# A two-layer attention, RWKV and retention block: RWKV work moved up, its products kept adjacent, and the planner's durations replaced

## The chip, the cores and the metric

The kernel runs on one core of a Trainium2 chip. A core has five engines that run their own instruction streams: TensorE (PE, matmuls and transposes), VectorE (DVE), ScalarE (ACT), GpSimd (POOL) and SyncE (SP, which issues the transfers here). The metric is the device time of one execution in microseconds (us), as the median of several runs. One further execution was recorded by the hardware profiler; every duration and wait below comes from it.

## The reference

The input x has 256 tokens of 1024 numbers, in float32. Two layers run one after the other. Each layer is

```
h = rms(x) * norm1_g
aq, ak, av, rw, rq, rk, rv, rg, gates = split(h @ w_in)
o_a = sliding_window_attention(rms(aq)*g, rms(ak)*g, av, sinks) @ w_attn_o   # 8 heads, 2 kv heads, window 128
o_b = rwkv7_time_mix(rw, ...) @ w_rwkv_o                                     # 8 heads of 64
o_c = retention(rotary(rq), rotary(rk), rv, silu(rg)) @ w_ret_o              # 8 heads of 64
x = x + (sigmoid(gates) mixes o_a, o_b, o_c) @ w_out
x = x + (silu(h2 @ w_ffn_gate) * (h2 @ w_ffn_up)) @ w_ffn_down               # h2 = rms(x) * norm2_g
```

The RWKV branch keeps a 64x64 state S per head. With one step per token it computes S = S * w + (S a) b + v k and y = S r. The result is normalized per head, and then

```
y = y * lnx_g + lnx_b
y = (y + bonus) * g          # bonus = sum(r * k * r_k) * v,  g = sigmoid(gd) @ g2
```

## The kernel before

Tokens stand in two blocks of 128 (t = 0 and 1). Weights are streamed once, in 292 units of 512 KB (`wunit`). Each unit arrives by a transfer into `raw`; ScalarE rounds it into `wh`, VectorE forms the rest `wl = raw - wh`, and the big matmuls use both halves: three matmuls (`wh,hth`, `wl,hth`, `wh,htl`) for one product in higher precision. There are three buffers for each of raw, wh and wl. These big matmuls are called bulk. They are chained in program order: rq, rk and the other input projections first, then the gate projection gt, in between the output projections of attention (`po<-wh,oah` and its two companions), of retention (`po<-wh,och`) and of RWKV (`po<-wh,obh`), then w_out and the feed-forward part.

All else in a layer's first half, the mixer, is small work of three branches, each with a stream number: RWKV is stream 1, retention 2, attention 3, and gates with the mixing of the three outputs 4.

- Attention of a block: scores `pas`; VectorE adds the mask (`sc<-pas`), takes maxima (`amx`) and their negatives (`anm`); ScalarE forms exponentials; `adn` is their inverted sum; the normed scores are transposed (`ptp`) and multiplied by the values (`poa`), which gives `oah` and `oal` for the output projection.
- Retention of a block: `pst`, masked into `sT`, `po<-rv_sb,sT` and `po<-Rz,rqT`; then squares `rsq`, sums `rvr`, a power on GpSimd (`rrr`), two products into `o`, and transposes `ptc` that feed `och` and `ocl`.
- RWKV goes in chunks of 64 tokens. VectorE inverts 32x32 triangles in a loop of 31 steps, each a product `prod<-Y,Tt` and a sum `Tt<-Tt,prod`, and transposes the result into M and Tn; TensorE multiplies `pz<-Tn,GA` and `pm<-M,Zs`. Then four chunks follow one on the other: `pr` (state times inputs), `pu`, `pd` (the state's change), with copies and sums on ScalarE and VectorE in between (RS, SV, Sn), and `py`, whose sum is `ysb`. The end normalizes ysb, applies lnx, bonus and gate (`pgt`), and transposes (`pto`) into `obh` and `obl`.

The program does not issue instructions as it is written. It records every operation (`Program`), and a planner (`schedule`, `forward`) then lays them out by a list schedule: at each step it takes from the ready operations of the engine that is free first the one of highest priority. The priority is the longest path to the end (`bl`), from estimated durations (`cost`) and hand-over times (`LAT_*`), with classes above it for weight units that are due and for bulk. An operation whose tile finds no free buffer is parked. PSUM has four banks for bulk (`psg`) and four for small results (`pss`). `emit` (line 421, in the changed kernel 431) issues all instructions, so every row of the profile shows that line, and rows are told apart by their tiles. What the planner writes is one fixed order for each engine; on the chip each engine runs its own in that order and waits where an input isn't there.

Of the kernel before, what the change touches and what calls it, by code (L numbers as in the profile page):

```python
# [19 lines left out]
T = 256  # L20
# [87 lines left out]
class Program:  # L108
# [48 lines left out]
    def cost(self, eng, method, args, kw, out, ins):  # L157
        n = 1
        for _, c in list(out.ap)[1:]:
            n *= c  # L160
        if eng == "PE":
            if method == "transpose":
                return 109
            if kw["lhsT"].dtype == F32R:
                return 3 + n / 2.4
            c = max(4 + 4 * n / 2.4, 60)
            return c if out.ap[0][1] > 64 else (0.67 if out.ap[0][1] > 32 else 0.36) * c
        src = any(_psum(a) for a in ins)
        if eng == "DVE":
            if method == "reciprocal":  # L170
                return 69 + 6.3 * n
            if method == "tensor_reduce":
                n = 1
                for _, c in list(ins[0].ap)[1:]:
                    n *= c
            if method in ("tensor_copy", "tensor_scalar", "memset") and not src:
                return 69 + n / 1.92
            return 69 + n / 0.96
        if eng == "ACT":
            c = (51 if src else 94) + n / 1.2  # L180
            if _is_ap(kw.get("scale", 1.0)) or _is_ap(kw.get("bias", 0.0)):
                c += 25 if kw["func"] == AF.Copy and not src else 93
# [16 lines left out]
    def add(self, eng, method, fn, args, kw):  # L199
# [37 lines left out]
        if merged is not None:  # L237
            assert merged["eng"] == eng
            merged["calls"].append((fn, args, kw))
            merged["touch"].update(touched)  # L240
            merged["cost"] += cost
            return
        if self.bundle:
            self.bundle[0] = i
        self.ops.append(dict(eng=eng, calls=[(fn, args, kw)], preds=preds, touch=set(touched),
                             cost=cost, method=method, bulk=self.bulk and eng == "PE",
# [17 lines left out]
    def schedule(self):  # L264
# [15 lines left out]
        for i in range(n - 1, -1, -1):  # L280
            bl[i] = ops[i]["cost"] + max((bl[j] + l for j, l in succ[i]), default=0.0)
        return self.forward(succ, need, bl)

    def forward(self, succ, need, bl):
# [12 lines left out]
        ready = {e: [] for e in wait}  # L297
        parked = {}
        tfree = {e: 0.0 for e in wait}
# [20 lines left out]
        def blocked(i):  # L320
# [6 lines left out]
            for (k, q), ts_ in new.items():  # L327
# [101 lines left out]
def hybrid_kernel(ctx: ExitStack, tc: tile.TileContext, A: dict, cst_d: bass.AP, out: bass.AP, layers=L):  # L429
# [229 lines left out]
    for l in range(layers):  # L659
# [136 lines left out]
        def rwkv_rest():  # L796
# [44 lines left out]


            GA = RT([128, 4, 4, 64], "GA")
            GR = RT([128, 4, 4, 64], "GR")
            gm = C("gmask")
            for p in range(4):
# [15 lines left out]
            BKT = [RT([128, 2, 4, 128], "BKT") for _ in range(2)]  # L862
            for i in range(2):
                for src in (na, EN):
                    pt = PS([128, 2, 2, 128], "ptb")
                    for j in range(2):
                        for d in range(2):
                            P.transpose(pt[:, j, d, :], src[:, 2 * i + j, d * 128:(d + 1) * 128], ident)
                    for par in range(2):
                        o_ = HR[par] if src is na else HR[1 - par]  # L870
                        cs = slice(64 * par, 64 * par + 64)
                        for ci in range(2):
                            S.copy(BKT[i].rearrange("p j (d c) v -> p j d c v", c=2)[o_, :, :, ci, cs], pt[HR[ci], :, :, cs])


# [50 lines left out]

            rk = RT([128, 4, T], "rk")
            for p in range(4):
                stt(rk[:, p, :], zr[:, p, :], vcol("rk", p), k2[:, p, :], MUL, MUL)
            pbs = head_sums(rk, "pbs")  # L930
            bsum = TL(sm_p, [128, 2, 8], F32, tag="bsum", name="bsum")
            S.copy(bsum.rearrange("p t (a b) -> p t a b", b=2), pbs)


            ysb = [RT([128, 8, 64], "ysb") for _ in range(2)]
            Sn = None
            for c in range(4):
# [3 lines left out]
                pr = PS([128, 4, 64], "pr")  # L941
                for p in range(4):
                    for par in range(2):
                        mm(pr[HR[par], p, :], X[p][:, par, c, 0:64], sv[:, p, par, :])
                RS = ST([128, 4, 64], "RS")
# [5 lines left out]
                pu = PS([128, 4, 64], "pu")  # L951
                for p in range(4):
                    for par in range(2):
                        mm(pu[HR[par], p, :], M[HR[par], p, c, :], RS[HR[par], p, :])
                S.copy(ysb[t][rr], py[rr])
                S.copy(sv[HR[0], :, 0, :], pu[HR[0]])
                S.copy(sv[HR[1], :, 1, :], pu[HR[1]])
                if c < 3:
                    pd = PS([128, 4, 64], "pd")
                    for p in range(4):  # L960
                        for par in range(2):
# [21 lines left out]
            lnx = MT([128, 2, 512], "lnx")  # L983
            rec.after = rec.latest(1)
            dma(out=lnx[:, 0, :], in_=bcast_rows(A["rwkv_lnx_g"], 512, l * 512))
            dma(out=lnx[:, 1, :], in_=bcast_rows(A["rwkv_lnx_b"], 512, l * 512))
            rec.after = None
            ob.extend([None, None])
            obh = TL(r_p, [128, 4, T], F32R, tag="r", name="obh")
            obl = TL(r_p, [128, 4, T], F32R, tag="r", name="obl")  # L990
            ob[:] = [obh, obl]
            for t in range(2):
# [12 lines left out]
                G.tensor_tensor(out=gr[:, :, 0], in0=vr[:, :, 0], in1=C("mh")[:, :8], op=ALU.pow)  # L1005
                bv = ST([128, 8, 64], "bv")
                tt(bv, vt[:, t, :].rearrange("p (h v) -> p h v", h=8), bc(bsum[:, t, :].unsqueeze(2), [128, 8, 64]), MUL)
                bvf = bv.rearrange("p h v -> p (h v)")
                tt(bvf, bvf, lnx[:, 1, :], ADD)
# [313 lines left out]
```

## Time and profile before

| | |
|---|---|
| median of 3 runs | 1000.04 us (999.21 to 1001.67) |
| profiled execution | 997.55 us, its span 995.7 us, mean granted TensorE clock 0.995 |
| mixer of layer 0, from the start to the first feed-forward matmul | 0 to 309.5 us |
| mixer of layer 1 | 497.8 to 804.4 us |
| busy: TensorE, VectorE, ScalarE, GpSimd | 968.9, 678.8, 525.7, 40.0 us |
| moved by transfers | 159 MB |

The span is the time from the first to the last instruction that the profile shows. The profiled execution is 1.85 us longer, and the median 2.49 us longer still. A row of a timeline has the start, the length, the engine, the line, the operation with its output and inputs, how many instructions it sums up, and in brackets how long the engine was idle before and what ended that.

### The profile page before, as it was taken

Reading aid. Unit: us, or ns where it says so; the run is one execution under the profiler, and the core shown is the slowest. Engines: PE = TensorE matmul, PEld = TensorE weight load, DVE = VectorE, ACT = ScalarE, POOL = GpSimd, SP = SyncE. Lnnn points to the kernel's source line nnn. Section 1 sums busy time; section 2 is a strip of 40 time slices with the busy share of each in tenths; the row PEclk is TensorE's granted clock in tenths of the full one; section 3 lists DMA queues with packets and bytes.
Section 4 is the critical chain, followed back from the end, with each engine's and each line's share of the span. In section 5 each row is a group of like instructions: output and inputs, shape, how many; then the busy total and the mean of one; then the engine's idle time right before and its main releaser. Section 6 shows DMA issues by size and latency. Waiting matters only on the chain.

```text
span 995.7 us, 15100 instructions
## 1 busy us (share of the span) xinstructions
PE 968.9 (97%) x5894; PEld 801.6 (81%) x5894; DVE 678.8 (68%) x1054; ACT 525.7 (53%) x828; POOL 40.0 (4%) x37
## 2 busy tenths in 40 slices
PE   8999999999899999999999999999996999999998
PEld 7998778878588888898889977688774888888886
DVE  5789968995766555555477998489846675555443
ACT  6756676445347444444366556844552474444432
POOL 1012001000100000000001010010001000000000
PEclk9999999999999999999999999999997999999999
DMA  7645533553346666655654544436621456666562
GB/s 240 183 149 172 163 111 128 165 155 105 112 155 184 178 188 190 188 173 187 190 170 148 165 137 129 143 107 189 191 66 64 151 172 196 184 188 188 175 207 104
DMA packets 93265, 159.04 MB, mean 160 GB/s; under 512 B 5798, under 2 KB 26506, under 8 KB 93194
## 3 DMA queue, kind: packets, MB, share of 16 engines
q1 hardware_dynamic: 93194, 158.08, 52.3%
q8 instruction: 46, 0.75, 0.3%
q14 instruction: 25, 0.20, 0.1%
HBM read 157.01 MB, written 1.05 MB: 159 GB/s over the span
## 4 chain that ended last, share of the span: by engine, by line
PE 84%; DVE 9%; ACT 4%; issue 2%; DMA 1%; POOL 1%; ACTq 0%; DVEq 0%; SPq 0%; POOLq 0%
PE pd L421 13%; PE pfg L421 12%; PE pfu L421 12%; PE gt L421 11%; PE po L421 7%; PE pf L421 6%; PE px L421 4%; DVE wl L421 3%; PE rv L421 2%; PE rg L421 2%; PE rq L421 2%; PE py L421 1%; DVE X L421 1%; ACT sc L421 1%; ACT wh L421 1%
## 5 line engine op out<-in xcount | busy, mean ns | idle before, releaser
L421 DVE TENSOR_TENSOR wl<-raw,wh 128x1024 fp32r<-128x1024 f32 x292 | 356.8, 1223 | 245.7 <-ACT wh L421 244.7
L421 ACT CAST wh<-raw 128x1024 fp32r<-128x1024 f32 x292 | 306.4, 1051 | 322.8 <-PE pd L421 67.5
L421 PE MATMUL gt<-wl,hth 128*128 128x512 f32 x192 | 77.3, 403 | 0.4 <-DVE wl L421 0.4
L421 PE MATMUL gt<-wh,htl 128*128 128x512 f32 x192 | 77.2, 402 | 0.0
L421 PE MATMUL gt<-wh,hth 128*128 128x512 f32 x192 | 76.5, 398 | 0.0
L421 PE MATMUL pfg<-wh,htl 128*128 128x512 f32 (+1 forms) x192 | 72.3, 377 | 0.0
L421 PE MATMUL pfg<-wl,hth 128*128 128x512 f32 (+1 forms) x192 | 72.3, 376 | 0.0
L421 PE MATMUL pfg<-wh,hth 128*128 128x512 f32 (+1 forms) x192 | 71.7, 374 | 0.0
L421 PE MATMUL pfu<-wh,hth 128*128 128x512 f32 (+1 forms) x192 | 71.3, 371 | 0.0
L421 PE MATMUL pfu<-wl,hth 128*128 128x512 f32 (+1 forms) x192 | 71.3, 371 | 0.0
L421 PE MATMUL pfu<-wh,htl 128*128 128x512 f32 (+1 forms) x192 | 71.3, 371 | 0.0
L421 PE MATMUL pd<-wl,ath 128*128 128x512 f32 x176 | 69.8, 396 | 0.0
L421 PE MATMUL pd<-wh,atl 128*128 128x512 f32 x176 | 69.7, 396 | 0.0
L421 PE MATMUL pd<-wh,ath 128*128 128x512 f32 x176 | 69.6, 395 | 0.0
L421 PE MATMUL pf<-hth,wl 128*128 128x256 f32 x224 | 64.0, 286 | 0.0
L421 PE MATMUL pf<-htl,wh 128*128 128x256 f32 x224 | 63.8, 285 | 0.0
L421 PE MATMUL pf<-hth,wh 128*128 128x256 f32 x224 | 63.5, 284 | 0.0
L421 PEld LDWEIGHTS gt<-wl,hth 128*128 128x128 f32 x192 | 36.1, 188 | 9.0 <-DVE wl L421 1.2
L421 PEld LDWEIGHTS pf<-htl,wh 128*128 128x128 f32 x224 | 42.9, 191 | 0.4 <-issue 0.3
L421 PEld LDWEIGHTS pf<-hth,wh 128*128 128x128 f32 x224 | 42.9, 191 | 0.1
L421 PEld LDWEIGHTS pf<-hth,wl 128*128 128x128 f32 x224 | 42.9, 191 | 0.0
L421 PEld LDWEIGHTS gt<-wh,htl 128*128 128x128 f32 x192 | 36.1, 188 | 7.4 <-issue 0.4
(322 smaller groups left out, 1951.9 us busy)
## 6 DMA issues: line engine op xcount, KB each, us to landing
raw<-in_w_in_dram SPq DMA_DIRECT2D x120, 512.0 KB, 3.8
raw<-in_w_ffn_gate_dram SPq DMA_DIRECT2D x44, 512.0 KB, 3.8
raw<-in_w_ffn_up_dram SPq DMA_DIRECT2D x44, 512.0 KB, 3.7
raw<-in_w_ffn_down_dram SPq DMA_DIRECT2D x44, 512.0 KB, 3.6
raw<-in_w_out_dram SPq DMA_DIRECT2D x16, 512.0 KB, 3.6
raw<-in_w_attn_o_dram SPq DMA_DIRECT2D x8, 512.0 KB, 3.6
raw<-in_w_ret_o_dram SPq DMA_DIRECT2D x8, 512.0 KB, 4.2
raw<-in_w_rwkv_o_dram SPq DMA_DIRECT2D x8, 512.0 KB, 3.7
```

The costliest lines, as they stand in the source:

```text
L421: fn(*args, **kw)
```

## The change

Nine edits go in together.

1. The planner's hand-over times fall from 130, 150, 250 and 400 ns to 45, 60, 160 and 310 ns, and its durations are replaced by ones taken from records: for instance 150 + n/0.96 ns for a VectorE operation on n elements, where 69 + n/0.96 stood.
2. `CROWD`: in the priority, durations of RWKV's small operations count 2.5 times.
3. Banks are reserved: when an operation that needs several tiles of the small PSUM banks finds too few, ready operations of other streams with lower priority may not take any.
4. The transposes that form BKT, and the products rk, pbs and bsum, are written ahead of the GA, GR and pg stage.
5. The eight products of each pr, pu and pd are bundled (`together`), so that nothing comes between them.
6. The second copy from pu into SV is done by VectorE instead of ScalarE.
7. The transfers of lnx may start once the recurrence begins, instead of after its last VectorE operation.
8. The gate's product pgt is formed ahead, and with it `ag = lnx_g * pgt` and `bg = (bonus + lnx_b) * pgt`.
9. The end is then y * ag, times the norm, plus bg, where it was y times the norm, times lnx_g, plus bonus, times pgt.

The arithmetic is the same apart from rounding. The core of the diff:

```
-LAT_SAME, LAT_X, LAT_IN, LAT_SIDE, LAT_OUT, LAT_DMA, LAT_ISSUE = 130, 150, 250, 400, 200, 930, 1290
+LAT_SAME, LAT_X, LAT_IN, LAT_SIDE, LAT_OUT, LAT_DMA, LAT_ISSUE = 45, 60, 160, 310, 200, 930, 1290
+CROWD = 2.5
...
-                return 3 + n / 2.4
+                return 13.5 + n / 2.4
...
-            return 69 + n / 0.96
+            return (210 if method == "scalar_tensor_tensor" else 150) + n / 0.96
...
-            c = (51 if src else 94) + n / 1.2
+            c = (155 if src else 200) + n / 1.2
...
-            bl[i] = ops[i]["cost"] + max((bl[j] + l for j, l in succ[i]), default=0.0)
+            crowd = CROWD if ops[i]["stream"] == 1 and not ops[i]["bulk"] else 1.0
+            bl[i] = crowd * ops[i]["cost"] + max((bl[j] + l for j, l in succ[i]), default=0.0)
...
                 if len(free[k]) < taken[k]:
+                    if ops[i]["wide"]:
+                        short.add(i)
+                    return k
+                if any(bl[j] > bl[i] and ops[j]["stream"] != ops[i]["stream"] for j in parked.get(k, ()) if j in short):
                     return k
...
-                for p in range(4):
-                    for par in range(2):
-                        mm(pr[HR[par], p, :], X[p][:, par, c, 0:64], sv[:, p, par, :])
+                with rec.together():
+                    for p in range(4):
+                        for par in range(2):
+                            mm(pr[HR[par], p, :], X[p][:, par, c, 0:64], sv[:, p, par, :])
...
-                S.copy(sv[HR[1], :, 1, :], pu[HR[1]])
+                V.tensor_copy(sv[HR[1], :, 1, :], pu[HR[1]])
...
+                pgt = PS([128, 512], "pgt")
+                mm(pgt, sg[:, t * 128:(t + 1) * 128], g2)
...
+                tt(a_[:, 0], lnx[:, 0, :], pgt, MUL)
+                tt(a_[:, 1], bvf, pgt, MUL)
...
+                tt(yf, yf, ag[t], MUL)
                 tt(y, y, bc(gr, [128, 8, 64]), MUL)
-                tt(yf, yf, lnx[:, 0, :], MUL)
-                tt(yf, yf, bvf, ADD)
-                pgt = PS([128, 512], "pgt")
-                mm(pgt, sg[:, t * 128:(t + 1) * 128], g2)
-                tt(yf, yf, pgt, MUL)
+                tt(yf, yf, bg[t], ADD)
```

The order of instructions moves at many places. Three of layer 0 are shown; layer 1 has them too. First TensorE where the attention of the second block is transposed (`ptp`). Before:

```order
L421 MATMUL ptp<-cst,sc 128x128 x4
L421 MATMUL gt<-wh,hth 128x512
L421 MATMUL gt<-wl,hth 128x512
L421 MATMUL gt<-wh,htl 128x512
L421 MATMUL gt<-wh,hth 128x512
L421 MATMUL ptp<-cst,sc 128x128 x8
```

Now, the last gt and what follows:

```order
L431 MATMUL gt<-wh,htl 128x512
L431 MATMUL po<-wh,oah 128x512
L431 MATMUL po<-wl,oah 128x512
L431 MATMUL po<-wh,oal 128x512
L431 MATMUL ptp<-cst,sc 128x128 x15
L431 MATMUL poa<-pT,kv 64x256
L431 MATMUL ptp<-cst,sc 128x128
L431 MATMUL poa<-pT,kv 64x256 x7
L431 MATMUL pst<-rqT,rkT 128x128 x8
L431 MATMUL po<-wh,oah 128x512
```

The transposes stood among gate matmuls; now they stand in one run, right before the part of the attention's output projection that needs their result. Between the last pas of the block and the first ptp there are now 14 gt, three po and one group of pg and pgk.

VectorE in the same stretch now takes the triangular loop between the attention's operations (anm, aes, adn):

```order
L431 TENSOR_REDUCE amx<-sc 128x4 x2
L431 TENSOR_TENSOR GA<-pg,cst 128x256
L431 TENSOR_TENSOR anm<-amx,arq 128x8
L431 STREAM_TRANSPOSE Y<-GA 128x1024
L431 TENSOR_TENSOR wl<-raw,wh 128x1024
L431 COPY Tt<-cst 128x32
L431 TENSOR_TENSOR anm<-anm,snk 128x8
L431 TENSOR_TENSOR prod<-Y,Tt 128x31
L431 TENSOR_TENSOR aes<-snk,anm 128x8
L431 TENSOR_TENSOR Tt<-Tt,prod 128x31
```

Before, the loop began only after this block's attention was done on VectorE; what has moved is the loop, past the attention's adn, oal and the retention's sT.

Second, TensorE from the retention's transposes ptc to pz. Now:

```order
L431 MATMUL po<-rv_sb,sT 128x64 x2
L431 MATMUL gt<-wl,hth 128x512
L431 MATMUL gt<-wh,htl 128x512
L431 MATMUL po<-wh,och 128x512
L431 MATMUL po<-wl,och 128x512
L431 MATMUL po<-wh,ocl 128x512
L431 MATMUL ptc<-cst,o_504 128x128 x4
L431 MATMUL po<-wh,och 128x512
L431 MATMUL po<-wl,och 128x512
L431 MATMUL pz<-Tn,GA 32x32 x13
```

Before, 41 bulk matmuls stood between that last sT product and ptc, and pz came in one run of 32 much later. VectorE now issues M and Tn right behind the second product of that retention block:

```order
L431 TENSOR_TENSOR o_504<-po,rrr 128x512
L431 TENSOR_TENSOR Tt<-Tt,prod 128x31
L431 TENSOR_TENSOR o_504<-o_504,rg_sb 128x512
L431 STREAM_TRANSPOSE M<-Tt 128x32x2x16
L431 STREAM_TRANSPOSE Tn<-Tt 128x32x2x16
L431 TENSOR_TENSOR ocl<-ptc,och 128x4x128
```

Before, the retention was long done when M and Tn came (only weight and gate operations stood beside them).

Third, TensorE at the end of the RWKV branch. Before:

```order
L421 MATMUL gt<-wh,htl 128x512
L421 MATMUL pto<-cst,ysb 128x128
L421 MATMUL pgt<-g_139,sg 128x512
L421 MATMUL pto<-cst,ysb 128x128 x3
L421 MATMUL po<-wh,obh 128x512
L421 MATMUL po<-wl,obh 128x512
L421 MATMUL pto<-cst,ysb 128x128 x4
L421 MATMUL po<-wh,obl 128x512
```

Now:

```order
L431 MATMUL gt<-wh,hth 128x512
L431 MATMUL pto<-cst,ysb 128x128 x4
L431 MATMUL gt<-wl,hth 128x512
L431 MATMUL gt<-wh,htl 128x512
L431 MATMUL gt<-wh,hth 128x512
```

The pto stood behind the last gt and right before the RWKV's output projection; now some 20 gt stand between the two runs of pto, and some 35 behind the second. The products pgt are issued before all of that.

More of the change, by code (lines that the diff above doesn't have):

```diff
@@ L175, in cost @@
                     n *= c
+            if method in ("transpose", "tensor_tensor_scan"):
+                return 150 + n / 0.5
             if method in ("tensor_copy", "tensor_scalar", "memset") and not src:
-                return 69 + n / 1.92
-            return 69 + n / 0.96
+                return 150 + n / 1.92
+            return (210 if method == "scalar_tensor_tensor" else 150) + n / 0.96
         if eng == "ACT":
-            c = (51 if src else 94) + n / 1.2
+            c = (155 if src else 200) + n / 1.2
             if _is_ap(kw.get("scale", 1.0)) or _is_ap(kw.get("bias", 0.0)):
-                c += 25 if kw["func"] == AF.Copy and not src else 93
+                c += 95
             if kw.get("accum_out") is not None:
@@ L240, in add @@
             merged["touch"].update(touched)
+            merged["wide"] = sum(self.tiles[t][0][0] == "pss" for t in merged["touch"]) > 1
             merged["cost"] += cost
@@ L244, in add @@
             self.bundle[0] = i
-        self.ops.append(dict(eng=eng, calls=[(fn, args, kw)], preds=preds, touch=set(touched),
+        self.ops.append(dict(eng=eng, calls=[(fn, args, kw)], wide=False, preds=preds, touch=set(touched),
                              cost=cost, method=method, bulk=self.bulk and eng == "PE",
@@ L297, in forward @@
         ready = {e: [] for e in wait}
-        parked = {}
+        parked, short = {}, set()
         tfree = {e: 0.0 for e in wait}
@@ L840, in rwkv_rest @@
                     tt(X[p][r_, par, :, 64:128], c4(zr[r_, p, :]), EI[r_, p, :, 1:65], MUL)
+            BKT = [RT([128, 2, 4, 128], "BKT") for _ in range(2)]
+            for i in range(2):
+                for src in (na, EN):
+                    pt = PS([128, 2, 2, 128], "ptb")
+                    for j in range(2):
+                        for d in range(2):
+                            P.transpose(pt[:, j, d, :], src[:, 2 * i + j, d * 128:(d + 1) * 128], ident)
+                    for par in range(2):
+                        o_ = HR[par] if src is na else HR[1 - par]
+                        cs = slice(64 * par, 64 * par + 64)
+                        for ci in range(2):
+                            S.copy(BKT[i].rearrange("p j (d c) v -> p j d c v", c=2)[o_, :, :, ci, cs], pt[HR[ci], :, :, cs])
+            rk = RT([128, 4, T], "rk")
+            for p in range(4):
+                stt(rk[:, p, :], zr[:, p, :], vcol("rk", p), k2[:, p, :], MUL, MUL)
+            pbs = head_sums(rk, "pbs")
+            bsum = TL(sm_p, [128, 2, 8], F32, tag="bsum", name="bsum")
+            S.copy(bsum.rearrange("p t (a b) -> p t a b", b=2), pbs)
             GA = RT([128, 4, 4, 64], "GA")
@@ L860, in rwkv_rest @@
                     tt(X[p][q_, par], pgk[q_], bc(gm[q_].unsqueeze(1), [64, 4, 128]), MUL)
[L862 to L868, printed above, removed]
-                    for par in range(2):
[L870 to L873, printed above, removed]
             Y = RT([128, 32, 32], "Y")
@@ L925, in rwkv_rest @@
                 G.memset(SV[0][HR[par], 0, :, par, :], 0.0)
-            rk = RT([128, 4, T], "rk")
-            for p in range(4):
[L929 to L932, printed above, removed]
+            begun = rec.latest(1)
             ysb = [RT([128, 8, 64], "ysb") for _ in range(2)]
@@ L941, in rwkv_rest @@
                 pr = PS([128, 4, 64], "pr")
-                for p in range(4):
-                    for par in range(2):
-                        mm(pr[HR[par], p, :], X[p][:, par, c, 0:64], sv[:, p, par, :])
+                with rec.together():
+                    for p in range(4):
+                        for par in range(2):
+                            mm(pr[HR[par], p, :], X[p][:, par, c, 0:64], sv[:, p, par, :])
                 RS = ST([128, 4, 64], "RS")
@@ L951, in rwkv_rest @@
                 pu = PS([128, 4, 64], "pu")
-                for p in range(4):
-                    for par in range(2):
-                        mm(pu[HR[par], p, :], M[HR[par], p, c, :], RS[HR[par], p, :])
+                with rec.together():
+                    for p in range(4):
+                        for par in range(2):
+                            mm(pu[HR[par], p, :], M[HR[par], p, c, :], RS[HR[par], p, :])
                 S.copy(ysb[t][rr], py[rr])
                 S.copy(sv[HR[0], :, 0, :], pu[HR[0]])
-                S.copy(sv[HR[1], :, 1, :], pu[HR[1]])
+                V.tensor_copy(sv[HR[1], :, 1, :], pu[HR[1]])
                 if c < 3:
                     pd = PS([128, 4, 64], "pd")
-                    for p in range(4):
+                    with rec.together():
+                      for p in range(4):
                         for par in range(2):
@@ L983, in rwkv_rest @@
             lnx = MT([128, 2, 512], "lnx")
-            rec.after = rec.latest(1)
+            rec.after = begun
             dma(out=lnx[:, 0, :], in_=bcast_rows(A["rwkv_lnx_g"], 512, l * 512))
@@ L987, in rwkv_rest @@
             rec.after = None
+            ag, bg = [], []
+            for t in range(2):
+                pgt = PS([128, 512], "pgt")
+                mm(pgt, sg[:, t * 128:(t + 1) * 128], g2)
+                bv = ST([128, 8, 64], "bv")
+                tt(bv, vt[:, t, :].rearrange("p (h v) -> p h v", h=8), bc(bsum[:, t, :].unsqueeze(2), [128, 8, 64]), MUL)
+                bvf = bv.rearrange("p h v -> p (h v)")
+                tt(bvf, bvf, lnx[:, 1, :], ADD)
+                a_ = RT([128, 2, 512], "ab")
+                tt(a_[:, 0], lnx[:, 0, :], pgt, MUL)
+                tt(a_[:, 1], bvf, pgt, MUL)
+                ag.append(a_[:, 0])
+                bg.append(a_[:, 1])
             ob.extend([None, None])
```

6 lines of the change are left out of this document (1 added, 5 removed).

## The prediction

> **What bounds the kernel now.** I read the page first (busy shares, then the slices), next what TensorE waits for, and last the timelines round each wait.
>
> ```profile
> span 995.7 us, 15100 instructions
> PE 968.9 (97%) x5894; PEld 801.6 (81%) x5894; DVE 678.8 (68%) x1054; ACT 525.7 (53%) x828; POOL 40.0 (4%) x37
> ```
>
> TensorE is the bound: 26.8 us of 995.7 are not busy. A reorder that adds and removes almost no matmuls can win those at most, and what a slower clock costs. The waits, by releaser (total, times, longest):
>
> ```profile
> PE pto L421 <- DVE ysb L421: 11.3, 4, 7.1
> ...
> PE pz L421 <- DVE Tn L421: 1.7, 2, 0.9
> ```
>
> So 11.3 us lie at the end of the two mixers, where the transposes pto wait for the RWKV output ysb. The longest wait, in layer 1, has a tail:
>
> ```profile
> 752.87 0.96 PE L421 MATMUL py<-SV,GR 64*64 64x64 f32 x16
> ...
> 761.99 0.47 PE L421 MATMUL pto<-cst,ysb 128*128 128x128 f32 x1 [7.11 <-DVE ysb L421]
> ...
> 765.74 1.12 PE L421 MATMUL pto<-cst,ysb 128*128 128x128 f32 x4 [0.93 <-DVE ysb L421]
> ...
> 767.51 0.63 PE L421 MATMUL po<-wh,obl 128*128 128x512 f32 x1
> 767.94 0.63 PE L421 MATMUL po<-wh,obh 128*128 128x512 f32 x1
> ...
> 770.64 0.40 PE L421 MATMUL po<-wh,obl 128*128 128x512 f32 x1
> 770.87 0.40 PE L421 MATMUL po<-wh,obh 128*128 128x512 f32 x1
> ```
>
> ```profile
> 766.00:768.00 2.00, 2.00 (x8) 0.50 0.00 0
> ...
> 770.00:772.00 2.00, 2.00 (x10) 1.00 0.00 0
> ```
>
> After the wait 512-wide matmuls start 0.43 us apart instead of 0.23, at a granted clock of 0.50 (fourth column of the window rows). Eight such matmuls (766.5 to 769.7) lose 8 x 0.20 = 1.6 us, and the gate products and transposes before them about as much of their 2.6 us as half the clock takes, 1.1 us: 2.7 us in all.
>
> **What the change removes.** In the new order 64 big matmuls (64 x 0.23 = 14.7 us) stand between the last py and the first pto. In the rows above first pto came 9.1 us after that py, the second four (765.74) 12.9 us after. Two of the vector operations in that chain go as well, since the gate's products are formed earlier. So all 11.3 us of pto waits go, and the 2.7 us of slow clock: the cover is the gate projection's bulk. The present 1.7 us before pz are counted as removed too, and priced anew below. Sum removed: 11.3 + 2.7 + 1.7 = **15.7 us**. The bounds: nothing, if the chain's new place is late by as much; and 26.8 + 2.7 = 29.5 us, if no idle time is left anywhere.
>
> Making pr, pu and pd adjacent and moving the second SV copy to VectorE I price at nothing. Every chunk of the recurrence has 4 to 13 bulk matmuls around those groups in both orders, which hide the copies; if that cover went, eight copies of about 0.4 us would be exposed, 3 us. The number of returns from small to bulk matmuls does not fall (158 before, 168 now, by the order). The lnx transfers issued earlier land long before use. One more vector operation per token block (0.6 us) lies beside the gate bulk.
>
> **What the change moves, and its price.** TensorE, VectorE and ScalarE each run their streams in order, so a producer's place in one stream and its consumer's in the other decide a wait. Three places got less cover, in both layers. My prices for TensorE:
>
> ```profile
> 127.05 0.28 PE L421 MATMUL pas<-klz,aqs 128*128 128x256 f32 x1
> ...
> 132.42 0.33 PE L421 MATMUL pg<-X,na 64*64 64x128 f32 x2
> ...
> 133.46 0.50 PE L421 MATMUL rg<-wh,hth 128*128 128x512 f32 x1
> ...
> 147.09 0.66 PE L421 MATMUL ptp<-cst,sc 128*128 128x128 f32 x4 [0.38 <-ACT BKT L421]
> ...
> 150.30 1.14 PE L421 MATMUL ptp<-cst,sc 128*128 128x128 f32 x8
> 151.20 0.47 PE L421 MATMUL gt<-wl,hth 128*128 128x512 f32 x1
> ...
> 152.07 2.00 PE L421 MATMUL poa<-pT,kv 128*64 128x256 f32 x16
> 154.00 0.44 PE L421 MATMUL ptb<-cst,na 128*128 128x128 f32 x2
> 154.37 1.16 PE L421 MATMUL pst<-rqT,rkT 64*128 64x128 f32 x16
> ```
>
> A pg/pgk group is 1.04 us (132.42 to 133.46), sixteen ptp 1.8 (twice 150.30 to 151.20), poa 1.93, pst 1.1, a bulk matmul 0.23. And for VectorE:
>
> ```profile
> 128.47 2.33 DVE L421 TENSOR_REDUCE amx<-sc 128x4 f32<-128x1024 f32 x2
> 130.72 0.41 DVE L421 TENSOR_TENSOR Rz<-pk,cst 64x256 f32<-64x256 f32 x1
> ...
> 196.45 0.42 DVE L421 TENSOR_TENSOR Tt<-Tt,prod 128x247 f32<-128x247 f32 x1
> 196.90 0.41 DVE L421 TENSOR_TENSOR prod<-Y,Tt 128x240 f32<-128x240 f32 x1
> ...
> 204.50 1.22 DVE L421 TENSOR_TENSOR wl<-raw,wh 128x1024 fp32r<-128x1024 f32 x1
> 205.64 0.36 DVE L421 TENSOR_TENSOR Tt<-Tt,prod 128x207 f32<-128x207 f32 x1
> ...
> 216.01 2.04 DVE L421 STREAM_TRANSPOSE M<-Tt 128x1024 f32<-128x1024 f32 x1
> 217.88 0.69 DVE L421 SCALAR_TENSOR_TENSOR tg<-tg,po 128x512 f32<-128x512 f32 x1
> 218.48 2.31 DVE L421 STREAM_TRANSPOSE Tn<-Tt 128x1024 f32<-128x1024 f32 x1
> 220.65 0.68 DVE L421 SCALAR_TENSOR_TENSOR tg<-tg,po 128x512 f32<-128x512 f32 x1
> ```
>
> ```profile
> L421 DVE TENSOR_TENSOR Tt<-Tt,prod 128x31 f32<-128x31 f32 (+15 forms) x62 | 21.1, 340 | 0.9
> ```
>
> From starts to starts: wl 1.14 us, a 512-wide operation 0.60, M 1.87, Tn 2.17 (Y, a third transpose of that size, is taken as 2.0), two amx 2.25. An operation of the triangular loop (prod and Tt in turn, each fed by the one before) takes its 0.34 us and 0.03 more.
>
> *Place a: the second token block's attention.* Its scores pas come some 100 bulk matmuls later than before relative to the weight stream, and the loop on VectorE has been moved up into the same stretch. Before, 20.0 us of other TensorE work lay between the last pas (127.05) and the first ptp (147.09). In the new order of layer 0, from the last pas to the first po that reads sT, TensorE has 25 bulk matmuls, a pg group, ptp, poa and pst: 5.75 + 1.04 + 1.8 + 1.93 + 1.1 = 11.6 us. VectorE must in that time do, in its order, the last sc, two X, oal and sT (5 x 0.60 = 3.0), amx 2.25, Y 2.0, two wl 2.3, GA and GR (half width, 0.33 each) 0.7, seven 8-wide ones of 0.1, and 34 of the loop's operations at 0.36 = 12.2: 23.1 us. The wait is 11.5 us. Layer 1 has 55 bulk matmuls and eight small pk there, 18.8 us, against 22.6 us on VectorE (five wl, 26 loop operations): 3.8 us. Together **15 us**. Bounds: 9.7, if loop operations start 0.25 apart, as where another stands between two; 19, if VectorE also idles 2 us in each layer for the exponentials on ScalarE. I take the sum, since rows give each of its parts.
>
> *Place b: the second block's retention output.* Between the last po (sT) and ptc, TensorE now has two gt and three po, 1.15 us; it had 41 bulk matmuls.
>
> ```profile
> 175.34 0.60 ACT L421 ACTIVATE rsq<-po 128x512 f32<-128x512 f32 x1 [1.91 <-PE po L421]
> ```
>
> ```profile
> 177.57 1.78 POOL L421 TENSOR_TENSOR rrr<-rvr,cst 128x8 f32<-128x8 f32 x1 [2.00 <-DVE rvr L421]
> ```
>
> ```profile
> 184.72 0.60 PE L421 MATMUL ptc<-cst,o 128*128 128x128 f32 x4
> ```
>
> The chain took 9.4 us (175.34 to 184.72), with a wl and others in between. Bare, it is 2.2 (175.34 to 177.57) + 1.78 + a 0.2 us rrr + two 512-wide operations 1.2 + about 0.3 of handing on, 5.7; two loop operations among them make 6.3. Less 1.15: 5.1 us a layer, **10.3 us**; between 9 (bare) and 16.5 (9.4 us again).
>
> *Place c: pz.* M and Tn now stand behind the second retention product on VectorE, and on TensorE four ptc (0.36) and two po (0.46) stand before pz. Wait: 1.87 + 2.17 + 0.1 - 0.8 = 3.3 us; in layer 1 six small loop operations (1.3 us) come before M too: 4.6. Together **7.9 us**, 5 if half of it overlaps, 9 at most.
>
> Sum added 15 + 10.3 + 7.9 = 33.2; net 33.2 - 15.7 = **+17.5 us**. The span becomes 1013.2, the profiled execution (997.55 for a span of 995.7) 1015.1, and the median, 2.5 above the profiled execution at 1000.04, 1017.5. Nothing gives these waits back: the bulk matmuls have one fixed order, the next ones at a are the attention's output projection and at b and c the retention's, which need the late results themselves, and TensorE is otherwise full.
>
> **The rivals.** *Slower clock behind the waits (1024).*
>
> ```profile
> 268.86 0.33 PE L421 MATMUL pto<-cst,ysb 128*128 128x128 f32 x1 [2.14 <-DVE ysb L421]
> ```
>
> ```profile
> 270.00:272.00 2.00, 1.11 (x6) 1.00 0.21 39
> ```
>
> The 7.1 us wait was followed by the slow clock, this one of 2.14 us in layer 0 was not (granted clock 1.00 behind it); the new waits in a and b lie between or above. At 2.7 us each, three more cost 8 us. Against it: in place a TensorE is not the bound just after it resumes, so its clock matters little there. The Trainium skill (TensorE: Matmul & The Clock Gate, Why this matters for your kernels) asks for no TensorE gaps above about 3 us, since one idle window brings the half clock back; by its window of about 3.4 us every wait in a and b would be charged 1.7 us, some 7 us in all, an estimate that comes out near this rival. The 7.1 us row agrees with it; the two tails show none of a length between 2.1 and 7.1.
>
> *The tails win (986).* The pto waits go and the middle stays covered: 1000 - 15.7 + 1.7. Its mechanism is at places a to c: VectorE and ScalarE reach sc, rsq and M with an empty queue, so that hand-over, not queue, sets each chain, and operations pipeline closer than their recorded lengths. It decides where the added waits fall below 15.7 us, under half my sum. For it: the present chains were long partly because VectorE worked on other things in between. Against it: the sums above hold starts to starts, and the loop alone, 62 x 0.34 = 21 us a layer, can't be taken out of the stretch.
>
> *They cancel (1000).* Added waits at their lower ends, 9.7 + 9 + 5 = 23.7, and 23 us won, which needs nearly all of TensorE's idle time to go, the first load's included.
>
> **How the numbers follow.** Forecast (1017): 0.62; slower clock: 0.18; tails win: 0.13; cancel: 0.07. The forecast's own range: 23.7 added and 20 won gives 1004, 44.5 (19 + 16.5 + 9) added and 15.7 won gives 1029. The range for 8 in 10, 1001 to 1030, leaves out most of the tails' case. About 0.3% is what a measurement here tells from no change: slower by more 0.79, within 0.08, faster 0.13.
>
> **What would show it.** TensorE's waits: pto gone; ptp or po waiting for ScalarE or VectorE in two spots of 4 to 12 us, the larger in layer 0; ptc for VectorE's o, 5 us twice; pz for Tn, 3 to 5 us, twice. The slices near 150 to 200 us and 650 to 700 us lose TensorE's nine tenths; the windows after a wait show the clock. In layer 0, pz starts within some 5 us of its present 220.9 though 100 fewer bulk matmuls precede it. I am wrong if ptp, ptc and pz together wait less than 16 us, or if pto still waits.

## The result: 1.2% slower, and the profile after

| | before | after |
|---|---|---|
| median | 1000.86 us (4 runs, 999.21 to 1001.71) | 1013.16 us (4 runs, 1011.38 to 1013.30) |
| profiled execution, its span | 997.55, 995.7 us | 1011.38, 1009.5 us |
| mean granted TensorE clock | 0.995 | 0.972 |

The ratio is 1.0121, 95% interval 1.0102 to 1.0140: slower by about 12 us. I had forecast 1017, in a range of 1001 to 1030.

The page of the changed kernel (busy shares, then the rows of TensorE and of its granted clock in 40 slices of 25.2 us):

```profile
span 1009.5 us, 15118 instructions
...
PE 974.3 (97%) x5894; PEld 807.8 (80%) x5894; DVE 689.0 (68%) x1066; ACT 522.7 (52%) x820; POOL 41.5 (4%) x37
...
PE   8999996979999999999999999988899999999998
...
PEclk9999997969999999999999999999799999999999
```

The holes stand in slices 7, 9 and 27 to 29, in the middle of the two mixers. Before, the one dip of the clock was at the end of the RWKV branch of layer 1. What TensorE waits for in the changed kernel (total, times, longest):

```profile
PE ptp L431 <- ACT sc L431: 9.5, 2, 8.1
PE ptc L431 <- DVE o L431: 8.6, 2, 4.3
PE pz L431 <- DVE Tn L431: 5.7, 2, 3.8
PE idle L431 <- POOL zero L431: 2.6, 1, 2.6
PE ptp L431 <- ACT pT L431: 2.1, 2, 1.2
...
PE po L431 <- DVE sT L431: 0.7, 1, 0.7
```

The 11.3 us of pto waits are gone. In their place stand 9.5 + 2.1 + 0.7 us at the second block's attention and sT, 8.6 at ptc and 5.7 at pz: 26.6 us. The largest, in layer 0, on three engines' timelines:

```profile
159.12 0.39 PE L431 MATMUL po<-wh,oal 128*128 128x512 f32 x1
167.56 1.97 PE L431 MATMUL ptp<-cst,sc 128*128 128x128 f32 x8 [8.06 <-ACT sc L431]
...
177.28 0.50 PE L431 MATMUL po<-wh,oah 128*128 128x512 f32 x1
```

```profile
161.60 0.60 ACT L431 ACTIVATE sc<-sc,anm,arq 128x256 f32<-128x256 f32 x1
...
166.20 0.19 ACT L431 ACTIVATION_READ_ACCUMULATOR sc<-sc,anm,arq 128x1 f32 x1
167.00 2.90 ACT L431 ACTIVATE sc<-sc,adn 128x256 f32<-128x256 f32 x7 [0.62 <-DVE adn L431]
```

```profile
157.69 2.02 DVE L431 STREAM_TRANSPOSE Y<-GA 128x1024 f32<-128x1024 f32 x1
...
166.41 0.17 DVE L431 TENSOR_TENSOR adn<-adn,aes 128x8 f32<-128x8 f32 x1 [0.42 <-ACT sc L431]
...
176.96 0.68 DVE L431 TENSOR_TENSOR oal<-poa,oah 128x512 fp32r<-128x512 f32 x1
...
177.89 0.68 DVE L431 TENSOR_TENSOR sT<-pst,cst 128x512 f32<-128x512 f32 x1
```

TensorE runs out of work that may go ahead at 159.5. The exponentials start only at 161.6, behind Y and a wl on VectorE, and take ScalarE until 166.4; VectorE then idles 0.42 us for them before adn, and the first normed scores come after 167. So of the 8.06 us 2.1 lie before the exponentials, 4.8 in them and 1.2 behind. VectorE reaches sT at 177.9, nearly 24 us after the last pas (154.1).

The second loss is not a wait. The granted clock (fourth column) in layer 0:

```profile
206.00:210.00 4.00, 0.00 (x0) 0.90 0.19 52
210.00:214.00 4.00, 1.94 (x6) 0.50 0.68 240
214.00:218.00 4.00, 3.97 (x54) 0.50 0.00 0
218.00:222.00 4.00, 4.00 (x32) 0.50 0.00 0
222.00:226.00 4.00, 4.00 (x71) 0.50 0.38 125
226.00:230.00 4.00, 4.00 (x31) 0.54 0.03 10
```

After the 4.33 us wait before ptc and the 1.87 before pz TensorE is busy again from 214 on, and works at half its clock until 229.7 (0.54 is the mean of 3.7 us at 0.50 and 0.3 at 1.00).

The start of the feed-forward part shows where the time was lost: its first matmul (pfg) starts at 323.62 in layer 0, where it started at 309.51, and at 818.18 in layer 1, where it started at 804.41. The changed kernel is 14.1 us behind at the first mark and 13.8 at the second, so layer 0 pays all of it. In layer 1 the new waits and the removed ones cancel.

### The profile page after: what moved, and what is told of

It reads as the page before. It is cut to its first block, busy times and chain, and to the rows that moved or that the text cites. A ratio compares the mean times of both kernels' runs of the same rounds, so it can differ in the third digit from the quotient of the medians.

```text
span 1009.5 us, 15118 instructions
## 1 busy us (share of the span) xinstructions
PE 974.3 (97%) x5894; PEld 807.8 (80%) x5894; DVE 689.0 (68%) x1066; ACT 522.7 (52%) x820; POOL 41.5 (4%) x37
## 3 DMA queue, kind: packets, MB, share of 16 engines
HBM read 157.01 MB, written 1.05 MB: 157 GB/s over the span
## 4 chain that ended last, share of the span: by engine, by line
PE 91%; DVE 4%; ACT 2%; DMA 1%; issue 1%; POOL 1%; ACTq 0%; POOLq 0%
PE gt L431 13%; PE pd L431 12%; PE pfg L431 12%; PE pfu L431 12%; PE po L431 8%; PE pf L431 7%; PE px L431 4%; PE rg L431 2%; PE rk L431 2%; PE aq L431 2%; PE rv L431 2%; PE py L431 1%; PE akv L431 1%; PE rq L431 1%; DVE wl L431 1%; PE ptf L431 1%
## 5 line engine op out<-in xcount | busy, mean ns | idle before, releaser
L431 PEld LDWEIGHTS gt<-wh,hth 128*128 128x128 f32 x192 | 36.1, 188 | 7.8 <-issue 0.6
```

The source lines that it names most:

```text
L431: fn(*args, **kw)
```

## The experiments

Four theories were tested. Theory 1: the new durations and hand-over times (edit 1) make the loss, the other edits gain. Theory 2: CROWD makes it. Theory 3: the half clock behind the waits is a cost of its own. Theory 4, formed after the first eight runs: within edit 1 it is VectorE's and ScalarE's durations. Ratios are to the kernel before, run beside each (medians 999.2 to 1000.5 us). Differences in us below are between medians; taken by the ratios they come out up to 2 us larger or smaller.

| run | edit, against | median, us | ratio (95%) |
|---|---|---|---|
| e1 | the change, edit 1 undone | 974.14 | 0.9733 (0.9693 to 0.9774) |
| e2 | before, with edit 1 alone | 1001.04 | 1.0009 (0.9990 to 1.0028) |
| e3 | the change, CROWD 1 | 1006.48 | 1.0064 (1.0038 to 1.0089) |
| e4 | the change, filled waits, first try | 1015.44 | 1.0145 (1.0109 to 1.0181) |
| e5 | the change, filled waits, second try | 1001.31 | 1.0019 (1.0008 to 1.0031) |
| e6 | the change, old durations | 981.75 | 0.9825 (0.9810 to 0.9839) |
| e7 | the change, old hand-over times | 988.98 | 0.9896 (0.9882 to 0.9911) |
| e8 | the change, edit 1 undone, CROWD 1 | **970.70** | 0.9719 (0.9704 to 0.9733) |
| e9 | e8 without bundles | 975.84 | 0.9765 (0.9734 to 0.9797) |
| e10 | before, with edits 7 to 9 alone | 989.79 | 0.9904 (0.9872 to 0.9936) |
| e11 | e8 with the new TensorE duration | 982.16 | 0.9829 (0.9790 to 0.9869) |
| e12 | e8 with the new VectorE and ScalarE durations | 1027.16 | 1.0281 (1.0245 to 1.0317) |

### Which edit: e1, e2, e3

**e1**, the change with the old numbers:

```
-LAT_SAME, LAT_X, LAT_IN, LAT_SIDE, ... = 45, 60, 160, 310, ...
+LAT_SAME, LAT_X, LAT_IN, LAT_SIDE, ... = 130, 150, 250, 400, ...
...
-                return 13.5 + n / 2.4
+                return 3 + n / 2.4
...
-            if method in ("transpose", "tensor_tensor_scan"):
-                return 150 + n / 0.5
...
-            return (210 if method == "scalar_tensor_tensor" else 150) + n / 0.96
+            return 69 + n / 0.96
...
-            c = (155 if src else 200) + n / 1.2
+            c = (51 if src else 94) + n / 1.2
...
```

> The change with the old durations and hand-over times (edit 1 undone, all else kept). In its order 75 bulk matmuls (17 us) stand between the last pas and the first ptp of the second block in layer 0, 102 in layer 1, and 69 or more between the last pr and pto. Theory 1 (edit 1 makes the loss, since its longer small durations let RWKV's path, counted 2.5 times, crowd out attention and retention; the other edits gain): no wait before ptp, ptc or pz over 3 us, none before pto, 980 to 991 us. Theory 2 (CROWD crowds them out whatever the durations are): 1008 us or more.

974.14 us: 39 us faster than the change, below the range of theory 1. Its TensorE waits:

```profile
PE pz L429 <- DVE Tn L429: 1.6, 2, 1.2
...
PE poa L429 <- ACT pT L429: 1.1, 1, 1.1
...
PE pto L429 <- DVE ysb L429: 0.5, 1, 0.5
```

Neither the tail's wait nor the middle's is left. Theory 2 falls: CROWD is 2.5 here.

**e2**, the kernel before with those lines the other way round:

> The kernel before with edit 1 alone. In its order no bulk matmul stands between the four pr of layer 0 and nine between those of layer 1, so each chunk's chain lies open: some 9 us a chunk less 4 of TensorE's own work, 5 x 8 = 40 us, less the 11 us of pto waits that it may share. Theory 1: 1025 to 1045 us. Theory 2 (edit 1 harmless by itself): within 5 us of 1000.

1001.04 us, no difference that this measurement tells. Theory 1's number was far off: I had taken a chunk of the recurrence to need 9 us, which is its pitch when bulk stands in it (pr starts at 228.34, 237.28 and 245.94 in the kernel before). The waits that the open recurrence makes are small:

```profile
PE pto L423 <- DVE ysb L423: 13.1, 4, 6.3
PE pr L423 <- DVE SV L423: 3.6, 4, 1.1
...
PE pd L423 <- ACT SV L423: 2.5, 5, 0.9
```

So edit 1 does not cost in the kernel before; it costs 39 us in the company of the other edits, and they without it gain 25.

**e3**, `CROWD = 1.0` in the change:

> The change with CROWD at 1 (edit 2 undone). Attention's second block is early again in layer 0, but 20 bulk matmuls stand between the first and last pr there, and three right before pto; in layer 1 ptp still follows its last pas by 64 bulk matmuls and pto stands next to the last pr. Theory 1: the recurrence lies open instead, 1010 to 1030 us. Theory 2 (CROWD is the loss): 980 to 992 us.

1006.48 us, 3.5 below theory 1's range and far above theory 2's. The wait at ptp goes, the one at pto comes back:

```profile
PE pto L431 <- DVE ysb L431: 12.9, 3, 6.2
PE ptc L431 <- DVE o L431: 4.6, 1, 4.6
```

With the new numbers and the two values of CROWD that were run, either the end of the recurrence or attention is late.

### The clock: e4, e5

**e4** puts matmuls of no use into three of the change's waits, when the order is issued:

```
+        fill = {('ptp', 8): 32, ('ptc', 4): 15, ('ptc', 12): 15}
...
+                                for _ in range(fill.get((k, seen[k]), 0)):
+                                    self.nc.tensor.matmul(args[0], lhsT=self.ident, rhs=self.ident, start=True, stop=True)
```

> The change with matmuls that do nothing of use put into three of its waits: 32 of 128x128 in float32 ahead of the second block's ptp in layer 0 (about 6.8 us at 0.21 each, of a wait of 8.06), 15 ahead of the second block's ptc in each layer (3.2 of 4.3 us). They write where the transposes write next. Theory 3 (the half clock behind the waits costs some 16 us: TensorE's work of 167 to 177, 210 to 228 and 707 to 721 us ran at half speed): granted clock near 1.00 there, 995 to 1000 us. Rival (what follows the waits is paced by the other engines, so the clock matters little): 1010 to 1014 us.

1015.44 us, a miss, by two faults of the experiment that its timeline shows:

```profile
163.65 10.27 PE L438 MATMUL ptp<-cst 128*128 128x128 f32 x64 [4.02 <-DVE X L440]
173.75 1.04 PE L440 MATMUL ptp<-cst,sc 128*128 128x128 f32 x8
```

```profile
213.39 0.66 PE L440 MATMUL ptc<-cst,o 128*128 128x128 f32 x4 [0.90 <-DVE o L440]
...
217.27 0.77 PE L440 MATMUL pz<-Tn,GA 32*32 32x32 f32 x26 [2.76 <-DVE Tn L440]
```

The fill at ptp had to wait for its PSUM bank until 163.65, ran at the half clock itself until 169.7, and let the transposes start 6.2 us later than in the change (173.75 against 167.56). The fill at ptc cost nothing, but the wait of 2.76 us before pz then brought the half clock by itself.

**e5** drops the fill at ptp, keeps the two at ptc and adds 10 and 15 matmuls before pz:

> The change again with idle matmuls in its waits, placed anew: 15 ahead of the second block's ptc in each layer (they took 3.5 us and delayed nothing), 10 (layer 0) and 15 (layer 1) ahead of the first pz, whose wait of 2.8 and 4.0 us was followed by the half clock in the run before this one; none at ptp. Theory 3 (the half clock behind the waits is a cost of its own): granted clock 1.00 from 206 to 232 us and from 703 to 735 us, pz to the first pr in 8 to 9 us instead of 14.5, and 1013 less 6 to 8 in layer 0 and 4 to 6 in layer 1: 999 to 1003 us. Rival (the stretch is paced by other engines): 1010 to 1014 us.

1001.31 us, as theory 3 expected. The same windows as above:

```profile
206.00:210.00 4.00, 4.00 (x34) 1.00 0.24 90
210.00:214.00 4.00, 3.09 (x27) 1.00 0.84 262
214.00:218.00 4.00, 3.46 (x69) 1.00 0.00 0
218.00:222.00 4.00, 4.00 (x92) 1.00 0.01 4
```

The stretch from the first ptc transpose to the first pr, in the change and then in e5:

```profile
210.22 1.09 PE L431 MATMUL ptc<-cst,o 128*128 128x128 f32 x4 [4.33 <-DVE o L431]
...
228.56 1.12 PE L431 MATMUL pr<-SV,X 128*64 128x64 f32 x16
```

```profile
211.03 0.66 PE L444 MATMUL ptc<-cst,o 128*128 128x128 f32 x4 [0.91 <-DVE o L444]
...
223.43 0.69 PE L444 MATMUL pr<-SV,X 128*64 128x64 f32 x16
```

From the first ptc transpose to the first pr layer 0 takes 12.4 us (211.03 to 223.43), where the change takes 18.3 (210.22 to 228.56); layer 1 takes 13.9 against 17.6. That is 9.6 us, where the medians differ by 11.9 (10 by the ratios) and the two traced executions by 9.4 of span (1009.5 and 1000.1), so these two places hold what e5 wins. The change as a whole lost 12.3. Nothing uses what the fill writes; the transposes and pz overwrite it.

### Which half of edit 1: e6, e7, e8

**e6** undoes the durations only (all of e1's diff but its first two lines), **e7** the hand-over times only:

```
-LAT_SAME, LAT_X, LAT_IN, LAT_SIDE, ... = 45, 60, 160, 310, ...
+LAT_SAME, LAT_X, LAT_IN, LAT_SIDE, ... = 130, 150, 250, 400, ...
```

> The change with the old durations but the new, shorter hand-over times. Its order has 60 bulk matmuls (13.8 us) from the last pas to ptp in layer 0, 83 in layer 1, and 46 to 54 from the last pr to pto. Theory 1a (of edit 1 the durations do the harm): 972 to 985 us. Theory 1b (the hand-over times do): 1000 us or more. Theory 1c (either half undone relieves it): below 995, and so does the next run.

> The change with the old hand-over times but the new durations. Its order has 53 and 41 bulk matmuls (12.2 and 9.4 us) from the last pas to ptp, and 71 and 51 from the last pr to pto. Theory 1a: 1000 us or more. Theory 1b: 972 to 985 us. Theory 1c: 984 to 995 us, with waits before ptp of some 2 and 5 us.

981.75 and 988.98 us: both below 995, as theory 1c has it. Neither half makes the loss alone in the company of CROWD 2.5: against e1 (974.14) the new hand-over times cost 7.6 us alone, the new durations 14.8 alone, and both together 39. With the new durations (e7) the waits at ptp are still there, 7.2 us; with the old ones (e6) none at ptp is over 0.8.

**e8** is e1 with

```
-CROWD = 2.5
+CROWD = 1.0
```

> The change with edit 1 undone and CROWD at 1. Its order has 67 and 61 bulk matmuls from the last pas to ptp, 54 and 58 from the last pr to the first pto, and pz stands 118 and 57 behind the second ptc. If the moved code, the reserve and the gate formed ahead carry the gain by themselves: 970 to 979 us, no wait above 2 us before pto, ptp, ptc. If CROWD is what pulls the recurrence off the end: 985 us or more, with pto waits.

970.70 us, the lowest of all and 42 below the change. It is 3.4 us below e1, but the intervals of the two ratios overlap. CROWD is not what gains.

```profile
span 968.7 us, 15117 instructions
...
PE 955.1 (99%) x5894; PEld 796.3 (82%) x5894; DVE 683.8 (71%) x1066; ACT 520.6 (54%) x820; POOL 42.3 (4%) x37
```

Its TensorE is idle for 13.6 us, 2.6 of them at the start, and busy for 13.8 us less than before with the same 5894 matmuls.

### What else gains: e9, e10

**e9** is e8 with, for pr, pu and pd alike,

```
-                with rec.together():
+                if True:
```

> The best version so far (the change with edit 1 undone and CROWD at 1) without the bundling of pr, pu and pd (edit 5 undone): bulk matmuls stand again inside these groups. Between the kernel before and that version TensorE's time on pr and pd fell by 1.5 us each and on gt by 4. If edit 5 earns that: 3 to 6 us slower than 970.7, so 974 to 977. My prediction's price (nothing): 969.5 to 972.

975.84 us, 5.1 us slower (4.6 by the ratios), in the range expected if the bundles earn it. The group of pr in e9, and then in e8:

```profile
L429 PE MATMUL pr<-SV,X 128*64 128x64 f32 x128 | 7.8, 230 | 0.0
```

```profile
L429 PE MATMUL pr<-SV,X 128*64 128x64 f32 x128 | 5.5, 228 | 0.0
```

The same 128 matmuls occupy 2.3 us less when nothing comes between them. No wait is shown in either: the cost lies in busy time (TensorE's whole busy time is 960.7 us in e9 and 955.1 in e8, its idle time 14.0 and 13.6).

**e10** is the kernel before with the gate formed ahead and lnx loaded early, edits 7 to 9:

```
-            rec.after = rec.latest(1)
+            rec.after = begun
...
+                tt(a_[:, 0], lnx[:, 0, :], pgt, MUL)
+                tt(a_[:, 1], bvf, pgt, MUL)
...
+                tt(yf, yf, ag[t], MUL)
                 tt(y, y, bc(gr, [128, 8, 64]), MUL)
-                tt(yf, yf, lnx[:, 0, :], MUL)
-                tt(yf, yf, bvf, ADD)
...
-                tt(yf, yf, pgt, MUL)
+                tt(yf, yf, bg[t], ADD)
```

> The kernel before with the gate formed ahead and lnx loaded early (edits 7 to 9 alone). Its order moves pto in layer 0 to 46 and 66 bulk matmuls behind the last pr, where it was 31; in layer 1 pto stays right behind the last pr. If the removed wait is mostly the position of pto, as I priced it: layer 0's 4 us go and layer 1's 8 shrink by the two or three vector operations taken out, 1.3 to 2: 993 to 996 us. If the shorter chain by itself does it: 984 to 988 us.

989.79 us, between the two expectations, 10.7 us faster than before.

```profile
PE pto L421 <- DVE ysb L421: 5.5, 1, 5.5
```

Of the 11.3 us, 5.5 stay, all in one wait, where layer 1 had 7.1 and 0.9: 2.5 us less, so that what was taken from the chain there is worth more than the 1.3 to 2 us I gave it. Which of the three edits earns what is not separated.

### Which durations: e11, e12

**e11** is e8 with TensorE's line of the new durations, **e12** is e8 with VectorE's and ScalarE's:

```
e11:
-                return 3 + n / 2.4
+                return 13.5 + n / 2.4
e12:
-            return 69 + n / 0.96
+            return (210 if method == "scalar_tensor_tensor" else 150) + n / 0.96
-            c = (51 if src else 94) + n / 1.2
+            c = (155 if src else 200) + n / 1.2
```

> The best version so far with TensorE's duration of edit 1 alone (13.5 ns more for each big matmul). Theory 4: what harms in edit 1 is that VectorE's and ScalarE's recorded durations are longer than the time until the next operation starts (0.68 against 0.60 us for a 512-wide one), so that the planner takes these two engines to be slower than they are; TensorE's new figure is close to its real pitch (0.227 to 0.23 us) and harmless. Its order has pz and pto some 115 bulk matmuls earlier in layer 0: 965 to 974 us. Rival (any longer durations bring the loss): 980 us or more.

> The best version so far with VectorE's and ScalarE's durations of edit 1 alone, TensorE's and the hand-over times old. Theory 4: the loss comes back; its order has 39 and 26 bulk matmuls between the first and last pr and pto right behind the last, so pto waits of 10 us or more, 990 to 1008 us. Rival (TensorE's duration is what harms): 968 to 976 us.

e12 gives 1027.16 us, above what theory 4 expected. e11 gives 982.16, which lies in the range of its rival (any longer durations bring the loss), so TensorE's figure is not harmless, as theory 4 had it. (The two lines for TensorE differ by 10.5 ns, not by the 13.5 of the expectation.) In this version VectorE's and ScalarE's durations cost 56 us, TensorE's 11. The waits of e12:

```profile
PE ptc L431 <- DVE o L431: 13.9, 3, 6.1
PE pto L431 <- DVE ysb L431: 11.9, 2, 6.2
PE rg L431 <- ACT q_sb L431: 5.0, 2, 4.6
PE ptp L431 <- ACT sc L431: 3.9, 1, 3.9
```

The 56 us are not the price of these durations in edit 1. With CROWD 2.5 all new durations together cost 14.8 us beside the old hand-over times (e1 to e7) and 31.4 beside the new ones (e6 to the change). In e2 the new durations and hand-over times cost nothing. And e7, which has e12's durations and hand-over times, TensorE's new duration and CROWD 2.5, is 38 us faster than e12; that difference is not explained.

Nor are the two halves of edit 1 independent. In the prediction's rows a Tt of 247 elements lasts 0.42 us (196.45), and the prod that needs it starts 0.45 after it (196.90). Between two such operations of one engine the planner counts the duration and LAT_SAME: 69 + 257 + 130 = 456 ns with the old numbers and 150 + 257 + 45 = 452 with edit 1's, but 537 in e7 and e12 and 371 in e6, which take only one of the two. So edit 1 leaves such chains about right. Yet e6 and e7 are faster than the change, so right chains alone do not make a good plan.

What edit 1 does lengthen are operations that need not wait for the one before. Two plain sums of 512 elements in the kernel before, what follows them, and their group:

```profile
222.35 1.32 DVE L421 TENSOR_TENSOR mix<-mix,tg 128x512 f32<-128x512 f32 x2
223.56 1.25 DVE L421 TENSOR_TENSOR wl<-raw,wh 128x1024 fp32r<-128x1024 f32 x1
```

```profile
L421 DVE TENSOR_TENSOR mix<-mix,tg 128x512 f32<-128x512 f32 x16 | 10.6, 688 | 0.0
```

One is recorded with 0.69 us, and the next operation starts 0.60 after it. The old figure, 69 + 512/0.96 = 602 ns, is the second number; the new one, 150 + 512/0.96 = 683 ns, is the first. For ScalarE:

```profile
140.31 1.99 ACT L421 CAST wh<-raw 128x1024 fp32r<-128x1024 f32 x2
```

Two casts in 1.99 us: one recorded with 1.05 and the other 0.94 ahead of it. The old figure is 94 + 1024/1.2 = 947 ns, the new 1053. The Trainium skill (Vector Engine (DVE) Microarchitecture Reference, Measured stream behaviour on trn2) gives about 75 ns for VectorE and 98 ns for ScalarE as the fixed cost of an instruction after overlap. The pitches here, some 70 and 90 ns above n/0.96 and n/1.2, agree nearly. The transposes M and Tn are the exception: 1.87 and 2.17 us from start to start, where the new figure is 150 + 1024/0.5 = 2198 ns and the old one 69 + 1024/0.96 = 1136.

So for most independent work the planner was told that two of its three busy engines are slower than they are. That this draws the small work out relative to bulk, until bulk reaches projections whose inputs are not there, fits the late ptp and ptc of e12 and of the change, and the late pto of e12; that the drawn-out plan is the mechanism is argued, not shown. A rival was not tested: the plan may be so sensitive that almost any change of its numbers away from the old ones moves the time by ten us and more. That TensorE's duration, which is close to its real pitch of 0.23 us, costs 11 us speaks for it. In e11 no wait is over 2.6 us; TensorE's shown waits and its busy time each grow by some 6 us.

## Why the prediction was right

**Direction, size and place.** The forecast was +17.5 us of span; it was +13.8, and +12.3 in the median. The three places were the right ones, and pto was gone.

**Place a** (15 us forecast). The size came near, in part by another path. VectorE took 23.8 us in layer 0 from the last pas (154.1) to sT (177.9), against 23.1 in my sum. The waits are 8.06 and 0.90 in layer 0, 1.41, 1.23 and 0.67 in layer 1: 12.3 us. But what ended the 8.06 us were the normed scores, with 4.8 us of exponentials on ScalarE before them that my sum leaves out (its upper bound has 2 us for them), and not VectorE's queue up to sT. The rest of that queue ran while TensorE was at half its clock: from 167.56 to 177.28, less the 0.90 us of wait, TensorE worked 8.8 us on what I had priced at 4.8. VectorE gave oal at 177.64, 0.2 us before `po<-wh,oal` (177.84), and had worked without a shown wait since 166.4. So at the full clock most of these 4 us would have been a wait for oal, as the rows have it (no run fills this wait in time), and I count them here: 16.3 us. In layer 1 the wait at ptp was not the 4 to 12 us of my signs but 1.4 and 1.2. My lower bound of 9.7 is a slip: 60 loop operations at 0.25 instead of 0.36 take 6.6 from 15.3 and leave 8.7.

**Place b** (10.3 us). 4.33 + 4.30 = 8.6. The chain took 5.5 us in layer 0 (rsq at 204.71, ptc at 210.22), where I had 6.3 with two loop operations, 5.7 bare: two loop operations do stand among the products, but each puts off the next by 0.12 us only (208.54 to 208.66, 209.27 to 209.38), and the others ran beside the power on GpSimd.

**Place c** (7.9 us). 1.87 + 3.81 = 5.7. In layer 0 the transposes ptc and two po before pz ran at the half clock, 1.9 us instead of 0.8, and covered more. pz starts at 214.0 in layer 0, 6.9 us earlier than before, where I had said within 5.

**The slow clock** is the step that failed. I priced it at nothing, on the ground that TensorE is not the bound just after it resumes, and left it to a rival at 8 us. The ground held at place a. Behind pz TensorE is the bound again, and the clock stayed down for 15.7 us more in layer 0 and 9.4 in layer 1. e5 shows 9.6 us in these two places: 5.9 and 3.7, where the rival had 2.7 for each of three dips. The rival had the right mechanism and nearly the right sum (its 8 us make 1025.5, not the 1024 that it is given).

**Removed, 15.7 us.** The pto waits and their dip went as said; and small waits of the first half that I did not count (1.2 before pw, 0.7 before po, several of 0.2 to 0.5) fell by 4.6 us too.

**Priced at nothing: adjacency.** e9 shows 5.1 us for the bundles, in the order of e8; in the change itself it was not measured. I had counted the returns from small to bulk matmuls, which do not fall, and not the small groups torn apart.

So three terms were mis-sized: the waits, with the slow stretch of place a, 33.2 against 30.6; the slow clock behind pz 0 against 9.6; and adjacency with the small waits 0 against some 10. The last two, both left out, nearly cancel. The three together take 3 us off the forecast's 17.5, and 13.8 were measured. That the total came near is in good part luck.

**The rivals.** That the tails win did not happen here, but its place is real: e10 has 10.7 us of it. None of the rivals, and nothing in the forecast, said that the change's own parts without the new numbers gain 25 to 29 us. My upper bound of what could be won, 29.5 us, was TensorE's idle time and the clock's loss. e8 wins 28.5, and of the 27.0 us that its span is shorter 13.8 are busy time, of which I had counted only the 2.7 us of the dip.

## What to carry to other kernels

A planner wants the time until an engine can start the next operation, and the time until a result can be used, as two numbers. A recorded duration is not the first (0.69 us recorded, 0.60 to the next start) and close to the second (0.42 recorded, 0.45 to the operation that needs it). Durations and hand-over times belong together (here both pairs give a chain the same time), and the plan has to be timed: the new durations cost from nothing (e2, with the new hand-over times) to 56 us (e12), by what stood beside them. On in-order engines a reorder is priced by pairs: for each small result that the fixed bulk order needs, sum the producer engine's work between the two marks and set it against TensorE's work between the same marks. And not only a wait has a price, but the work behind it too: here that ran at half the clock for up to 15.7 us.

## What the runs showed of the hardware

- After waits of 8.1 us, 4.3 and 1.9, and 4.3 and 3.8 the granted clock was 0.50, and it stayed there although no further wait is shown: from 214.0 to 229.7 in layer 0 and from 711.9 to 721.2 in layer 1, with 32x32 and transposing matmuls among the bulk. Long waits are not needed for it. In e4 one of 2.76 us was enough, with a wait of 0.90 and 1.1 us of work before it. In the change two of 1.41 and 1.23 us were, with eight transposes between (0.50 from 666.6 to 670.0). At 550.6 the clock fell for 3.4 us with no wait over 0.4 us before it; there sixteen matmuls of two columns (pss) stood among the bulk within 3.1 us, which in the kernel before were spread over 5.7 and brought no fall. The 2.14 us before had brought none either.
- Read from windows of 2 us, the slow spells in the mixers of the change last 13.6 us (161.4 to 175.1), 20.5 (209.2 to 229.7), 3.4, 3.4 and 13.7 (707.6 to 721.2), that in the kernel before 10.2 (759.6 to 769.8): about 1, 3, 4 and 6 times 3.4. The Trainium skill (TensorE: Matmul & The Clock Gate, What's actually happening) has a free-running window of about 3.4 us, idle to slow down and busy to recover. The lengths agree with such a window. But waits shorter than the window that still slow the clock, and 9 to 16 us without a shown wait before recovery, are not what it gives if every busy microsecond counts; that the small and transposing matmuls count for less would fit, and no run varies them.
- Idle matmuls that wrote where the next transposes write kept the clock at 1.00 and delayed nothing where the bank was free (e5).
- Small matmul groups with other matmuls between them cost TensorE time that shows as busy: 7.8 us in e9 against 5.5 in e8 for 128 pr.
